# Merging three mixers' branches: later row preparation, a fixed place for one half, a pause before weight scales

## The chip, the cores and the metric

One core of a Trainium2 chip runs the program. The metric is device time in microseconds (us) of one execution. An execution was profiled as well; its span runs from its first to its last instruction.

## What is computed

One macaron block over 1024 tokens of width 1024 (`DEPTH` is 1), all in float32 at the interface:

```python
x = x + 0.5 * swiglu_ffn(rms_norm(x, ffn1_norm[l]), ffn1_w_in[l], ffn1_w_out[l])
h = rms_norm(x, mix_norm[l])
...
o_a = indexed_sparse_attention(...) @ w_o_a[l]
glu_a, glu_b = jnp.split(y_s @ w_glu[l], 2, axis=-1)
o_b = glu_a * jax.nn.sigmoid(glu_b)
o_m = memory_attention(q_m, m_k, m_v) @ w_o_m[l]
g = jax.nn.sigmoid(gates.reshape(b_, s_, N_BRANCHES, D_MODEL))
merged = g[:, :, 0] * o_a + g[:, :, 1] * o_b + g[:, :, 2] * o_m
x = x + merged @ w_out[l]
x = x + 0.5 * swiglu_ffn(rms_norm(x, ffn2_norm[l]), ffn2_w_in[l], ffn2_w_out[l])
x = rms_norm(x, final_norm[l])
```

The place that matters here is `merged` and the product with `w_out` behind it.

## The kernel before

Every operand of a product is held as two float16 halves, a high and a low one, each scaled by a power of two, and a product is three matmuls (`matmul3`): high by high, high by low, low by high. So weights and activations have to be split before TensorE can use them. For a weight block (`WBlock`) this is: load into the staging tile `wf`; square sums per block or per row (ACT writes `junk` and a sum, some on DVE); `weigh` (DVE, `wj`), which weighs the sums by what the activation rows were scaled with; `scale`, which begins with a matmul by ones (tile `ms`) that adds over partitions, and goes on with three to five tiny DVE steps (`wsc`, `wrs`); then the high half (ACT, `wh`) and the low half (DVE, `wh`). For activations, `Rows` does the same: `put(k, src)` starts a generator `steps` whose first part is the square sum on ACT (`junk` with `rsc`), the next, at a later call of `more()`, the power of two on DVE (`rsc`, `mi`, `mj`) and the high half on ACT (`m`), and the last the low half on DVE (`m`).

All instructions are recorded through one helper (line 62), so rows are told apart by tile names. The order on each engine is fixed when the program is built. Generators yield between pieces of TensorE work; a model of the engines' clocks (`Model`) decides which goes on (`Sched`), and after each step `Stream.prep` pushes the weight blocks ahead as far as the model thinks they are ready. `WBlock.can` allows `scale` only once the model's time is `LATE` past the end of the step before; `LATE` is 0.0 until the second FFN sets it to 2.5. Whoever needs a block whose steps have not been issued forces them with `go()` (in `Stream.begin`). On the chip each engine runs its own list in order.

**The merge** (in `mixer`). Channels come in 8 groups d of 128, tokens in 2 halves of 512: 16 units n = 2d + half. A unit has 30 matmuls of 512 columns: six into `gb` (bank tag `lg`), six into `ga` (`mm`), six into `pm` (`ao`), twelve into `po` (`mm`). ACT empties them: tanh of `gb` to `sb`, a copy of `ga` to `gc`, a copy of `pm` to `sm`; in the next unit, behind its first six matmuls, `rest` copies `po` to `m`, a place in `xa`. DVE multiplies `sb` by `gc` and by a gate, `sm` by its gate, `m` by its gate; POOL adds `sm` to `sb` and `sb` to `m`. The three gates come back from DRAM by a DMA on POOL's queue (`g_in`, two units ahead). Temporaries `sb`, `sm`, `gc` share a ring of four buffers (`t2`). Banks: `lg` 2, `mm` 2, `ao` 1, `ms` 3. After the second half of a d, `rest` puts row d into `w["m"]` at once, so the row's square sum stands on ACT right behind the copy of `po`.

`xa` is 16 places of 512 floats: gates in places 0 to 8, `m` in 9 to 14.

**The output projection** (`out_stage`). Weight blocks `out[0]` to `out[3]` of 256 columns (d = 0, 1; 2, 3; ...). The first two are cut into rows 0 to 5 and rows 6 and 7, so that the product can start without the last rows. Tiles go d0, d1, d2 for both halves, then d3 to d7 of half 0, then d3 to d7 of half 1; each is 18 + 6 or 24 matmuls, emptied by DVE into `xo` and `xa`, squared by ACT (`sq`) and summed by DVE (`ss`). `begun` calls `more()` after each pair of rows. Meanwhile the first blocks of the second FFN are prepared (`wf<-in_ffn_w_in_dram`, square sums `junk`), and `norm_forms` norms the finished half (DVE `xa`, ACT and DVE `F`).

Of the kernel before, what the change touches and what calls it, by code (L numbers as in the profile page):

```python
# [21 lines left out]
HT = 512  # L22
# [482 lines left out]
class Stream:  # L505
# [28 lines left out]
    def room(self):  # L534
        return len(self.ring) < 3 or self.ring[-3].uses == 0
# [24 lines left out]
class Rows:  # L560
# [6 lines left out]
        self.inv2 = kb.const.tile([P, nk], F32, name=tag + "j")  # L567
        self.n, self.at, self.late, self.apart = 0, {}, [], False

    def put(self, k, src, mul=None):  # L570

        self.late += [self.steps(k, src, mul)]
        self.more()

    def more(self):
# [4 lines left out]
        while self.late:  # L580
            self.more()

    def steps(self, k, src, mul):
        kb, nc = self.kb, self.kb.nc
        t = kb.small.tile([P, 3], F32, name="rsc", tag="rsc", bufs=4)
        hl = self.t[k] = self.room(k)
        nc.scalar.activation(kb.junk(S), src, AF.Square, accum_out=t[:, 0:1])
        yield None
        kb.pow2(t[:, 0:1], t[:, 1:2], t[:, 2:3])
        inv = self.inv[:, k:k + 1]  # L590
        if mul is None:
            nc.vector.tensor_scalar(inv, t[:, 1:2], INV_MUL, None, op0=OP.mult)
        else:
            nc.vector.tensor_scalar(inv, t[:, 1:2], INV_MUL, mul, op0=OP.mult, op1=OP.mult)
        nc.vector.tensor_tensor(self.inv2[:, k:k + 1], inv, inv, op=OP.mult)
        if self.apart:
            yield None
        nc.scalar.activation(hl[:, 0], src, AF.Copy, scale=t[:, 2:3])
        yield None
        nc.vector.scalar_tensor_tensor(hl[:, 1], src, t[:, 2:3], hl[:, 0], op0=OP.mult, op1=OP.subtract)  # L600
        self.n, self.at[k] = k + 1, nc.t["vector"] + 0.12
# [5 lines left out]
class Builder:  # L607
# [406 lines left out]
    def ffn_strassen(self, name, rows, a, b, F, ring, early, chunks, xd):  # L1014
# [42 lines left out]
        def body(s, then):  # L1057
# [5 lines left out]
            if late:  # L1063
                put(*late.pop())
# [94 lines left out]
        for f in range(PLAIN, NF):  # L1159
            s = s or (yield from first(f))  # L1160
            s = yield from body(s, none if f + 1 == NF or f in ends else lambda: first(f + 1))
            if f in ends:
                rows.flush()
                yield from out(b[ends.index(f)], *chunks[ends.index(f)])
        rows.flush()
        put(*late.pop())
        rows.flush()

# [1046 lines left out]
    def mixer(self, w, xa, ss, xd_in, xd_out, after):  # L2215
# [87 lines left out]
        heads = lambda t, half: lambda i, k: t[:, 4 * half:4 * half + 4, 2 * k + i]  # L2303
        gates, mt, xf = {}, {}, xa.rearrange("p k a h t -> p (k a h t)")
        room = lambda i, n: xf[:, i * HT:(i + n) * HT].rearrange("p (j t) -> p j t", j=n)

        def g_in(n):
            if n < 2 * ND:
                gates[n] = room(3 * (n % 3), 3)
                nc.gpsimd.dma_start(gates[n], gd[:, n // 2, n % 2].rearrange("j p t -> p j t"))  # L2310
# [5 lines left out]
        for n in range(2 * ND):  # L2316
            d, half = divmod(n, 2)
            b = w["go"][d // 2]
            glu, wm, wa = b.segs
            c = (d % 2) * P  # L2320
            yield from self.stream.begin(b)
            gb, ga = self.bank("lg"), self.mm()
            self.matmul3(gb, lambda i, k: glu.hl[:, i, k, 256 + c:256 + c + P], w["y"].x(half), 2)
            if late:
                late.pop()()
            yield None
            self.matmul3(ga, lambda i, k: glu.hl[:, i, k, c:c + P], w["y"].x(half), 2)
            sb, sm, gc = self.t2("sb"), self.t2("sm"), self.t2("gc")
            nc.scalar.activation(sb, gb, AF.Tanh, scale=glu.inv)
            yield None  # L2330
            w["m"].more()
            g_in(n + 2)
            ta, tg, tm = (gates[n][:, j] for j in range(3))
            pm, po = self.bank("ao"), self.mm()
            self.matmul3(pm, lambda i, k: wm.hl[:, i, k, c:c + P], heads(qmS, half), 2)
            nc.scalar.activation(gc, ga, AF.Copy, scale=glu.inv)
            nc.vector.scalar_tensor_tensor(sb, sb, 1.0, gc, op0=OP.add, op1=OP.mult)
            nc.vector.scalar_tensor_tensor(sb, tg, 1.0, sb, op0=OP.add, op1=OP.mult)
            yield None
            self.matmul3(po, lambda i, k: wa.hl[:, i, k, c:c + P], heads(qS, half), 4, ks=range(2))  # L2340
            nc.scalar.activation(sm, pm, AF.Copy, scale=wm.inv)
            nc.vector.scalar_tensor_tensor(sm, tm, 1.0, sm, op0=OP.add, op1=OP.mult)
            nc.gpsimd.tensor_tensor(sb, sb, sm, op=OP.add)
            w["m"].more()
            yield None
            self.matmul3(po, lambda i, k: wa.hl[:, i, k, c:c + P], heads(qS, half), 4, ks=range(2, 4))
            self.stream.end(b)
            if half == 0:
                mt[d] = room(9 + 2 * (d % 3), 2)

            def rest(d=d, half=half, wa=wa, po=po, ta=ta, sb=sb):
                m = mt[d][:, half]
                nc.scalar.activation(m, po, AF.Copy, scale=wa.inv)
                nc.vector.scalar_tensor_tensor(m, ta, 1.0, m, op0=OP.add, op1=OP.mult)
                nc.gpsimd.tensor_tensor(m, m, sb, op=OP.add)
                if half == 1:
                    w["m"].put(d, mt[d].rearrange("p h t -> p (h t)"))

            late.append(rest)
            yield None  # L2360
        w["out"][0].go(("split", 0))
        late.pop()()
        self.stream.BACKLOG = 3
        nc.free.add(xa.tensor.name)
        en.close()
# [212 lines left out]
```

## Time and profile before

| what | value |
|---|---|
| three runs, median (lowest to highest) | 2257.52 us (2257.22 to 2260.11) |
| the profiled execution, its own time | 2257.12 us |
| its span | 2255.0 us, 33448 instructions |
| mean granted TensorE clock | 0.988 |
| busy: PE, DVE, ACT, POOL | 2140.5, 1347.8, 1186.8, 396.2 us |
| HBM read and written | 143.57 and 40.50 MB, 82 GB/s over the span |

Names: PE is TensorE's matmuls, DVE VectorE, ACT ScalarE, POOL GpSimd, SP the queue of SyncE. In a timeline a row is: start in us from the span's start, how long, engine, line, operation, out<-in, shape, count, and in brackets how long the engine had been idle before it and who released it. In a list of waits the time is summed. A matmul's time in the timeline includes its drain, so that of a group overlaps the next.

### The profile page before, as it was taken

How to read it: one execution, taken by the hardware profiler on the slowest of the kernel's cores; microseconds unless marked ns; L12 is line 12 of the kernel's file. 1: busy time of each engine (PE TensorE's matmuls, PEld its weight loads, DVE VectorE, ACT ScalarE, POOL GpSimd, SP SyncE). 2: the span in 40 equal slices, each digit the busy share in tenths (PEclk: the TensorE clock that was granted, in tenths of full speed). 3: DMA queues.
4: the chain of work that ended last, by engine and by line, in shares of the span. 5: the costliest groups of instructions: out<-in, count | busy, mean ns of one | idle time of the engine just before them, and what ended most of it. 6: DMA issues, size and time to landing. Idle time of an engine off the chain costs nothing. (4 is left out here: it accounts for less than half of the span.)

```text
span 2255.0 us, 33448 instructions
## 1 busy us (share of the span) xinstructions
PE 2140.5 (95%) x12585; PEld 1141.1 (51%) x12589; DVE 1347.8 (60%) x3669; ACT 1186.8 (53%) x2367; POOL 396.2 (18%) x582
## 2 busy tenths in 40 slices
PE   6999999999999889979999999898999999999997
PEld 3555444444444556656556674333854444444443
DVE  6446852344555467677669886675756643466653
ACT  6543434344444488778877766544555432455421
POOL 1200130000000103312200004410254301344100
PEclk9999999999999999999999999999999999999999
DMA  6422231202222102123321204334111234112222
GB/s 224 120 82 82 64 103 57 63 26 80 89 89 85 52 20 79 40 66 108 122 86 58 65 37 152 117 120 119 43 57 57 70 123 125 47 57 64 81 62 93
DMA packets 204066, 185.18 MB, mean 82 GB/s; under 512 B 7376, under 2 KB 176528, under 8 KB 203264
## 3 DMA queue, kind: packets, MB, share of 16 engines
q1 hardware_dynamic: 185904, 135.84, 19.1%
q0 software_dynamic: 8416, 29.36, 4.1%
q10 hardware_dynamic: 9584, 17.85, 2.7%
q8 instruction: 98, 1.61, 0.3%
q14 instruction: 64, 0.52, 0.1%
HBM read 143.57 MB, written 40.50 MB: 82 GB/s over the span
## 5 line engine op out<-in xcount | busy, mean ns | idle before, releaser
L62 PEld LDWEIGHTS <-wh 128*128 128x128 f16 x8412 | 817.3, 98 | 949.5 <-issue 38.0
L62 PE MATMUL mm<-xa,wh 128*128 128x512 f16 x2376 | 540.0, 380 | 6.5 <-ACT xa L62 4.9
L62 PE MATMUL lg<-xa,wh 128*128 128x512 f16 x1080 | 242.6, 379 | 0.4 <-DVE xn L62 0.4
L62 ACT ACTIVATE junk<-wf 128x1024 f16<-128x1024 f32 (+3 forms) x292 | 194.0, 664 | 35.7 <-DMA wf<-in_ffn_w_in_dram 20.1
L62 PE MATMUL mm<-G,wh 128*128 128x512 f16 x960 | 210.5, 379 | 0.0
L62 DVE SCALAR_TENSOR_TENSOR wh<-wf,wsc,wh 128x1024 f16<-128x1024 f32 (+1 forms) x132 | 176.3, 1337 | 49.3 <-ACT wh L62 49.1
L62 PE MATMUL mm<-H,wh 128*128 128x512 f16 x864 | 197.3, 383 | 6.8 <-ACT wh L62 5.2
L62 PE MATMUL lg<-F,wh 128*128 128x512 f16 (+1 forms) x900 | 179.4, 353 | 0.0
L62 ACT ACTIVATE wh<-wf,wrs 128x128 f16<-128x128 f32 (+2 forms) x304 | 112.4, 438 | 103.4 <-DVE wrs L62 94.0
L62 ACT ACTIVATE wh<-wf,wsc 128x1024 f16<-128x1024 f32 (+1 forms) x132 | 139.1, 1060 | 33.3 <-DVE wsc L62 23.3
L62 PE MATMUL mm<-wh,xa 128*128 128x256 f16 (+2 forms) x1152 | 129.1, 271 | 13.9 <-ACT us L62 7.8
L62 PE MATMUL mm<-F,wh 128*128 128x512 f16 (+1 forms) x672 | 129.2, 347 | 0.0
L62 PEld LDWEIGHTS <-xa 128*128 128x128 f16 x1152 | 108.2, 106 | 32.1 <-issue 15.4
L62 DVE SCALAR_TENSOR_TENSOR wh<-wf,wrs,wh 128x128 f16<-128x128 f32 (+2 forms) x304 | 112.9, 423 | 12.7 <-ACT wh L62 11.5
L62 DVE SCALAR_TENSOR_TENSOR gt<-lg,wsc,si 128x512 f32<-128x512 f32 x44 | 33.0, 749 | 129.6 <-PE lg L62 110.5
L62 PE MATMUL ao<-F,wh 128*128 128x512 f16 x456 | 104.6, 379 | 0.0
L62 ACT ACTIVATE junk<-wk,kathr 128x1024 f16<-128x1024 f32 (+2 forms) x96 | 99.5, 1036 | 8.7 <-POOL kathr L62 6.8
L62 POOL TENSOR_TENSOR xa<-hs,xa 128x512 f16<-128x512 f32 x16 | 19.9, 1249 | 475.4 <-ACT xa L62 475.4
L62 DVE SCALAR_TENSOR_TENSOR xo<-mm,wsc,xo 128x512 f32<-128x512 f32 x44 | 33.0, 749 | 102.9 <-PE mm L62 102.9
L62 POOL TENSOR_TENSOR xa<-xa 128x512 f32<-128x512 f32 (+1 forms) x40 | 57.2, 1432 | 174.2 <-ACT xa L62 125.7
L62 ACT ACTIVATE junk<-gt 128x1024 f16<-128x1024 f32 x22 | 23.2, 1057 | 120.1 <-DVE gt L62 120.1
L62 PE MATMUL mm<-m,wh 128*128 128x512 f16 x336 | 79.9, 395 | 5.1 <-DVE wh L62 3.2
(511 smaller groups left out, 2924.8 us busy)
## 6 DMA issues: line engine op xcount, KB each, us to landing
wf<-in_ffn_w_in_dram SPq DMA_DIRECT2D x88, 512.0 KB, 4.8
xo<-xd ACTq DMA_DIRECT2D x64, 256.0 KB, 2.7
gd<-gt SPq DMA_DIRECT2D x48, 256.0 KB, 2.0
xa<-gd POOLq DMA_DIRECT2D x16, 768.0 KB, 5.0
wf<-in_ffn_w_out_dram SPq DMA_DIRECT2D x8, 1280.0 KB, 5.9
wf<-in_ffn_w_out_dram SPq DMA_DIRECT2D x7, 1408.0 KB, 5.9
wf<-in_w_in_dram SPq DMA_DIRECT2D x17, 512.0 KB, 4.8
xd<-xa SPq DMA_DIRECT2D x32, 256.0 KB, 2.4
```

Source lines behind the costliest of these rows:

```text
L62: r = f(*a, **k)
```

## The change

Rows are put two steps of a unit later (behind `sm` instead of behind the first six matmuls), `gc` gets place 15 of `xa` for its own instead of a buffer of the ring, the last row's first step waits for three more calls of `more()`, and `LATE` is set to 2.0 from unit 12 on and to 3.5 after the loop. The second FFN sets `LATE` to 2.5 in both kernels once its first three blocks are through.

```diff
@@ -567,9 +567,9 @@
         self.inv2 = kb.const.tile([P, nk], F32, name=tag + "j")
         self.n, self.at, self.late, self.apart = 0, {}, [], False
 
-    def put(self, k, src, mul=None):
-
-        self.late += [self.steps(k, src, mul)]
+    def put(self, k, src, mul=None, after=0):
+
+        self.late += [self.steps(k, src, mul, after)]
         self.more()
 
     def more(self):
@@ -580,8 +580,10 @@
         while self.late:
             self.more()
 
-    def steps(self, k, src, mul):
+    def steps(self, k, src, mul, after):
         kb, nc = self.kb, self.kb.nc
+        for _ in range(after):
+            yield None
         t = kb.small.tile([P, 3], F32, name="rsc", tag="rsc", bufs=4)
         hl = self.t[k] = self.room(k)
         nc.scalar.activation(kb.junk(S), src, AF.Square, accum_out=t[:, 0:1])
@@ -2303,6 +2305,7 @@
         heads = lambda t, half: lambda i, k: t[:, 4 * half:4 * half + 4, 2 * k + i]
         gates, mt, xf = {}, {}, xa.rearrange("p k a h t -> p (k a h t)")
         room = lambda i, n: xf[:, i * HT:(i + n) * HT].rearrange("p (j t) -> p j t", j=n)
+        spare, ready = xf[:, 15 * HT:16 * HT], []
 
         def g_in(n):
             if n < 2 * ND:
@@ -2319,13 +2322,15 @@
             glu, wm, wa = b.segs
             c = (d % 2) * P
             yield from self.stream.begin(b)
+            if n == 12:
+                WBlock.LATE = 2.0
             gb, ga = self.bank("lg"), self.mm()
             self.matmul3(gb, lambda i, k: glu.hl[:, i, k, 256 + c:256 + c + P], w["y"].x(half), 2)
             if late:
                 late.pop()()
             yield None
             self.matmul3(ga, lambda i, k: glu.hl[:, i, k, c:c + P], w["y"].x(half), 2)
-            sb, sm, gc = self.t2("sb"), self.t2("sm"), self.t2("gc")
+            sb, sm, gc = self.t2("sb"), self.t2("sm"), spare
             nc.scalar.activation(sb, gb, AF.Tanh, scale=glu.inv)
             yield None
             w["m"].more()
@@ -2342,6 +2347,8 @@
             nc.vector.scalar_tensor_tensor(sm, tm, 1.0, sm, op0=OP.add, op1=OP.mult)
             nc.gpsimd.tensor_tensor(sb, sb, sm, op=OP.add)
             w["m"].more()
+            if ready:
+                w["m"].put(*ready.pop())
             yield None
             self.matmul3(po, lambda i, k: wa.hl[:, i, k, c:c + P], heads(qS, half), 4, ks=range(2, 4))
             self.stream.end(b)
@@ -2354,12 +2361,14 @@
                 nc.vector.scalar_tensor_tensor(m, ta, 1.0, m, op0=OP.add, op1=OP.mult)
                 nc.gpsimd.tensor_tensor(m, m, sb, op=OP.add)
                 if half == 1:
-                    w["m"].put(d, mt[d].rearrange("p h t -> p (h t)"))
+                    ready.append((d, mt[d].rearrange("p h t -> p (h t)")))
 
             late.append(rest)
             yield None
         w["out"][0].go(("split", 0))
         late.pop()()
+        w["m"].put(*ready.pop(), after=3)
+        WBlock.LATE = 3.5
         self.stream.BACKLOG = 3
         nc.free.add(xa.tensor.name)
         en.close()
```

Three places show how the change moves instructions.

First, ACT in units 4 and 5 of the merge, before the change. `junk_14650,rsc_14648` is the square sum of row 1, `m_14649` its high half; `sb`, `gc`, `sm` are copies out of banks of unit 4, then of unit 5; `xa_91<-mm` is `rest`.

```order
L62 ACTIVATE xa_91<-mm_14610,wsc_12915 128x512
L62 ACTIVATE junk_14650,rsc_14648<-xa_91 128x1024
L62 ACTIVATE sb_14661<-lg_14637,wsc_13129 128x512
L62 ACTIVATE m_14649<-xa_91,rsc_14648 128x1024
L62 ACTIVATE gc_14663<-mm_14638,wsc_13129 128x512
L62 ACTIVATE sm_14662<-ao_14671,wsc_13245 128x512
L62 ACTIVATE xa_91<-mm_14672,wsc_13371 128x512
```

The same with the change (`gc` is now the `xa_91` that reads the bank filled by the second six matmuls: `mm_14634`, `mm_14697`):

```order
L62 ACTIVATE xa_91<-mm_14607,wsc_12915 128x512
L62 ACTIVATE sb_14653<-lg_14633,wsc_13129 128x512
L62 ACTIVATE junk_14658,wrq_14657<-wf_14423 128x512
L62 ACTIVATE xa_91<-mm_14634,wsc_13129 128x512
L62 ACTIVATE junk_14672,wrq_14657<-wf_14423 128x512
L62 ACTIVATE sm_14654<-ao_14661,wsc_13245 128x512
L62 ACTIVATE junk_14685,rsc_14683<-xa_91 128x1024
L62 ACTIVATE junk_14688,wss_14687<-wf_14423 128x512
L62 ACTIVATE xa_91<-mm_14662,wsc_13371 128x512
L62 ACTIVATE sb_14713<-lg_14696,wsc_13129 128x512
L62 ACTIVATE junk_14717,wss_14716<-wf_14423 128x1024
L62 ACTIVATE m_14684<-xa_91,rsc_14683 128x1024
```

The square sum of row 1 moved from in front of `sb` to behind `sm` of unit 4, its high half from in front of `gc` of unit 4 to in front of `gc` of unit 5.

Second, DVE at the end of tile d2 and around tile d3 of the projection, where block `out[2]` is scaled: before the change (`wj_15667` to `wrs_15675`, then `wh_15698`).

```order
L62 SCALAR_TENSOR_TENSOR wj_15667,wss_15578<-wrq_15579,mj_110 128x8
L62 TENSOR_SCALAR wsc_15669<-ms_15670 128x1
L62 TENSOR_SCALAR wsc_15669<-wsc_15669 128x1 x2
L62 TENSOR_SCALAR wrs_15675<-mi_109,wsc_15669 128x8
L62 SCALAR_TENSOR_TENSOR xo4_15399<-mm_15644,wsc_15476,xo4_15399 128x512
L62 SCALAR_TENSOR_TENSOR xa_91<-lg_15678,wsc_15570,xo4_15399 128x2x256
L62 TENSOR_TENSOR ss1_93<-ss1_93,sq_15688 128x512
L62 SCALAR_TENSOR_TENSOR wh_15698<-wf_15494,wrs_15675,wh_15698 128x256 x2
L62 SCALAR_TENSOR_TENSOR junk2_15713,wrq_15710<-wf_15612 128x256
L62 SCALAR_TENSOR_TENSOR xo4_15400<-mm_15691,wsc_15476,xo4_15400 128x512
```

With the change (`wj_15704` to `wrs_15716`, then `wh_15718`; `lg_15691` is the last bank before the block's first product):

```order
L62 SCALAR_TENSOR_TENSOR xo4_15401<-mm_15661,wsc_15309,xo4_15401 128x512
L62 SCALAR_TENSOR_TENSOR xa_91<-lg_15691,wsc_15509,xo4_15401 128x2x256
L62 TENSOR_TENSOR ss0_92<-ss0_92,sq_15701 128x512
L62 SCALAR_TENSOR_TENSOR wj_15704,wss_15594<-wrq_15595,mj_110 128x8
L62 SCALAR_TENSOR_TENSOR junk2_15708,wrq_15673<-wf_15544 128x256
L62 TENSOR_SCALAR wsc_15710<-ms_15711 128x1
L62 TENSOR_SCALAR wsc_15710<-wsc_15710 128x1 x2
L62 TENSOR_SCALAR wrs_15716<-mi_109,wsc_15710 128x8
L62 SCALAR_TENSOR_TENSOR wh_15718<-wf_15527,wrs_15716,wh_15718 128x256 x8
```

The scale of `out[2]` moved from two tiles ahead of the block's first product to behind the last tile before it.

Third, PE in the last two tiles, where the matmul by ones of an FFN block stands (`mm_16092` is tile d6 and `mm_16115` tile d7 of half 1). Before the change, after 18 of the 24 matmuls of tile d6:

```order
L62 MATMUL mm_16092<-m_15139,wh_15822 128x512
L62 LDWEIGHTS ones_b_76
L62 MATMUL ms_16120<-wss_16114,ones_b_76 128x1
L62 LDWEIGHTS ones_b_76
L62 MATMUL ms_16120<-wss_16114,ones_b_76 128x1
L62 LDWEIGHTS wh_15822
```

With the change, after 12 of the 24 matmuls of tile d7:

```order
L62 MATMUL mm_16115<-m_14952,wh_15812 128x512
L62 LDWEIGHTS ones_b_76
L62 MATMUL ms_16131<-wss_16098,ones_b_76 128x1
L62 LDWEIGHTS ones_b_76
L62 MATMUL ms_16131<-wss_16098,ones_b_76 128x1
L62 LDWEIGHTS wh_15812
```

The pair moved back by 6 + 12 = 18 matmuls. The next pair moved by 24 and the one after it by 48 matmuls of 256 columns; behind PE's row 18200 or so (the fourth FFN block) both lists are the same.

## Rows read from the trace of the kernel before

**Rows 1.** The page, part 1: busy us, share, instructions.
```profile
PE 2140.5 (95%) x12585; PEld 1141.1 (51%) x12589; DVE 1347.8 (60%) x3669; ACT 1186.8 (53%) x2367; POOL 396.2 (18%) x582
```

**Rows 2.** Windows: stretch, length, busy us by engine (x), clock, DMA.
```profile
1352.70:1471.00 118.30, 105.35 (x489) 46.83 (x487) 81.86 (x143) 66.97 (x117) 57.38 (x43) 1.00 0.39 129
...
1558.00:1577.00 19.00, 10.25 (x39) 4.43 (x39) 9.22 (x15) 7.83 (x12) 2.31 (x2) 0.73 0.19 55
```

**Rows 3.** Waits of PE, 1352 to 1497 us: total, times, longest.
```profile
PE mm L62 <- ACT gc L62: 9.8, 6, 2.7
```

**Rows 4.** Waits of PE, 1497 to 1645 us.
```profile
PE ms L62 <- ACT junk L62: 10.9, 5, 7.7
```

**Rows 5.** Timeline of PE in the merge: units 0, 1, 5, the end.
```profile
1352.67 1.46 PE L62 MATMUL lg<-y,wh 128*128 128x512 f16 x6
...
1359.15 1.46 PE L62 MATMUL lg<-y,wh 128*128 128x512 f16 x6
...
1387.67 1.46 PE L62 MATMUL mm<-y,wh 128*128 128x512 f16 x6 [1.11 <-ACT gc L62]
...
1471.01 1.24 PE L62 MATMUL mm<-m,wh 128*128 128x512 f16 x5
```

**Rows 6.** Timeline of ACT in the merge: unit 1, unit 4.
```profile
1363.32 0.69 ACT L62 ACTIVATE sm<-ao,wsc 128x512 f32<-128x512 f32 x1 [0.69 <-PE ao L62]
...
1384.28 1.06 ACT L62 ACTIVATE junk<-xa 128x1024 f16<-128x1024 f32 x1 [4.77 <-POOL xa L62]
...
1386.95 0.67 ACT L62 ACTIVATE gc<-mm,wsc 128x512 f32<-128x512 f32 x1
```

**Rows 7.** Timeline of DVE in the merge.
```profile
1360.07 0.69 DVE L62 SCALAR_TENSOR_TENSOR xa<-xa 128x512 f32<-128x512 f32 x1 [1.56 <-ACT xa L62]
...
1389.66 1.28 DVE L62 SCALAR_TENSOR_TENSOR m<-xa,rsc,m 128x1024 f16<-128x1024 f32 x1
...
1390.85 1.76 DVE L62 SCALAR_TENSOR_TENSOR xa<-xa 128x512 f32<-128x512 f32 x1
```

**Rows 8.** Timeline of POOL in the merge.
```profile
1360.90 1.27 POOL L62 TENSOR_TENSOR xa<-xa,sb 128x512 f32<-128x512 f32 x1 [1.05 <-DVE xa L62]
...
1389.84 2.23 POOL L62 TENSOR_TENSOR sb<-sb,sm 128x512 f32<-128x512 f32 x1 [4.85 <-DVE sm L62]
```

**Rows 9.** Timeline of PE, start of the projection.
```profile
1476.30 7.90 PE L62 MATMUL mm<-m,wh 128*128 128x512 f16 x28 [2.84 <-DVE wh L62]
...
1484.62 1.46 PE L62 MATMUL mm<-m,wh 128*128 128x512 f16 x6 [0.42 <-DVE xo L62]
```

**Rows 10.** Timeline of PE, first products of block out[2].
```profile
1515.68 6.94 PE L62 MATMUL mm<-m,wh 128*128 128x512 f16 x30 [0.61 <-ACT wh L62]
...
1522.46 0.17 PE L62 MATMUL ms<-wss,ones_b 128*128 128x1 bf16 x1
```

**Rows 11.** Timeline of DVE at that place.
```profile
1513.81 0.75 DVE L62 SCALAR_TENSOR_TENSOR xa<-lg,wsc,xo 128x512 f32<-128x512 f32 x1 [0.54 <-PE lg L62]
...
1515.26 0.69 DVE L62 TENSOR_TENSOR ss<-ss,sq 128x512 f32<-128x512 f32 x1 [0.69 <-ACT sq L62]
```

**Rows 12.** Timeline of ACT, first high halves of out[3].
```profile
1523.40 0.91 ACT L62 ACTIVATE wh<-wf,wrs 128x256 f16<-128x256 f32 x2 [1.92 <-DVE wrs L62]
```

**Rows 13.** Timeline of PE, end of the projection and second FFN.
```profile
1565.73 0.16 PE L62 MATMUL ms<-wss,ones_b 128*128 128x1 bf16 x1 [7.75 <-ACT junk L62]
...
1566.91 0.16 PE L62 MATMUL ms<-wss,ones_b 128*128 128x1 bf16 x1 [1.02 <-ACT junk L62]
...
1566.94 9.49 PE L62 MATMUL mm<-m,wh 128*128 128x512 f16 x30
...
1594.68 0.16 PE L62 MATMUL ms<-wss,ones_b 128*128 128x1 bf16 x1 [0.95 <-ACT junk L62]
...
1597.71 2.62 PE L62 MATMUL mm<-F,wh 128*128 128x256 f16 x12
```

**Rows 14.** Timeline of DVE, the emptying of tile d5 of half 1.
```profile
1562.20 0.74 DVE L62 SCALAR_TENSOR_TENSOR xa<-mm,wsc,xo 128x512 f32<-128x512 f32 x1
```

## The prediction

> **What bounds the kernel.** I read the page first, then PE by stretches, then the waits of PE, then single rows. PE is busy for 95% of the span [rows 1], so the time is what PE works plus what it waits; a change that adds no matmul can only move the waits. In the merge PE works 105.4 of 118.3 us [rows 2]. The list of waits names the cause: PE stood 9.8 us, in six pieces, for ACT's copy `gc` [rows 3], and later 10.9 us for ACT's square sums of weights [rows 4]. The order of ACT's list says why, and the rows say how much.
>
> **1. The merge.** A unit takes PE 1359.15 - 1352.67 = 6.48 us when nothing is in its way [rows 5]: 30 matmuls, 0.216 us each. Sixteen make 103.7 us; the stage took 1471.01 - 1352.67 = 118.3 [rows 5]. So 14.6 us are lost. The row of unit 4 shows how: ACT stood 4.77 us before the square sum of row 1, for POOL's last addition [rows 6], and behind it in the list were `sb`, the high half and `gc`, which ended at 1386.95 + 0.67 = 1387.6. PE began the second six matmuls of unit 5 at 1387.67, 1.11 us late [rows 5]. Unit 4 began at 1352.67 + 4 x 6.48 = 1378.6, so the row was ready 5.7 us into the unit. With about 3.3 us of ACT work up to the end of `gc` and PE asking 7.8 us into the unit (6.48 + 1.30), anything later than 4.5 stops PE.
>
> The change puts the square sum behind `sm`. In an undisturbed unit (start 1359.15) `sm` starts 4.2 us in [rows 6] and POOL's addition to `m` ends at 1360.90 + 1.27 [rows 8], 3.0 us in: the row is there before ACT asks. What now stands behind the square sum is the copy of `po`, wanted 10.4 us in (6.48 and 18 matmuls), and after the DVE's scale step and the high half the `gc` of the next unit, wanted 14.3 us in (12.96 + 1.30). From the square sum to the end of that `gc` I count some 6 us, so the row may be ready 8 us into the unit, not 4.5. The place of its own for `gc` adds no instruction; it takes `sm`'s wait for POOL's addition out, as two units now share the ring of four. Its reuse is safe by some 5 us: DVE has read it about 4.1 us into a unit (12 matmuls, 2.6, then a copy and a product of 0.7 each) and ACT writes it again 9.2 us in.
>
> What is left is DVE. One of its operations took 1.76 us while POOL was at work, against 0.69 alone [rows 7], and POOL's 2.23 against 1.27 [rows 8]; they take turns. Two units hold on DVE eight operations of 0.69, one of 1.28 [rows 7] and small ones of some 0.6, and on POOL four of 1.27: 5.5 + 1.3 + 0.6 + 5.1 = 12.5 us if none overlap, of 12.96 us on PE. Weight halves come on top, so DVE falls back by a few us in units 5 to 9 and 14 to 15, within the 8 us allowed. I leave 2.0 us of waits: **gain 12.6** (14.6 if DVE keeps up; 6.6 if 8 us stay, about half).
>
> **2. Into the projection.** From 1471.01 [rows 5] to 1484.62 [rows 9] PE did 36 matmuls, 7.8 us of work, in 13.6: 5.8 lost, to a wait of 2.84 for low halves of `out[0]`, one before it, one of 0.42 and 28 matmuls that took 7.90 instead of 6.05 + 0.17 us [rows 9]. With the change those low halves for rows 0 to 3 stand earlier, but I find four new short waits by laying the new lists beside the durations of rows 6 to 8: `gc` of unit 15 behind the high half of row 6, which waits for DVE (2.1 us until its bank is free for the first tile); rows 4 and 5 of `out[0]`, whose low halves stand behind the low half of row 6 (1.5); the first tile, emptied behind four low halves of `out[1]` (1.2); an `lg` bank (0.9). The last row, three calls later, adds nothing: its square sum waits for POOL either way, and its first user is six matmuls behind the fourth tile. Sum 5.7: **gain 0.1** (5.8 if none comes; -2 if a further wait of the size of [rows 9] does).
>
> **3. Block `out[2]`.** This is the price of the longer `LATE`. PE waited 0.61 us here [rows 10]. Now the block's `wj` stands on DVE behind the emptying, square and sum of the last tile before it, and PE's matmul by ones right before the block's first product. From the end of that tile: 0.2 until DVE starts, 1.45 to the start of `ss` [rows 11], 0.6 for it, 0.25 for `wj`, 0.1 to PE, 0.94 from the matmul by ones [rows 10] to ACT's first high half [rows 12], 0.45 for that: 4.0 us instead of 0.8. Behind a long wait PE starts slowly: 1.7 us more for 28 matmuls [rows 9], 9.49 - 6.65 = 2.8 us more for 30 after 8.8 us of waiting [rows 13], in a stretch whose granted clock was 0.73 [rows 2], part of it at 1.2 GHz; after 1.11 us nothing [rows 5]. I take 1.8. **Loss 5.0** (3.2 to 6.0). The Trainium skill (TensorE: Matmul & The Clock Gate, Part 1) says that an idle array falls to half its clock and gets it back by work; by that rule 4.0 us would cost as the longest wait does, 2.8, and the loss be 6.0.
>
> **4. Block `out[3]`.** Its matmul by ones stands 6 instead of 12 matmuls ahead, 1.3 us, and 0.94 + 0.45 are needed; later rows queue behind a tile's square as before. **Loss 0.7** (0 to 1.5).
>
> **5. Third FFN block.** The pair by ones waited 7.75 + 1.02 us [rows 13], because its square sums stand on ACT behind the norm of half 0. It moves back 18 matmuls, 3.9 us. Not all helps: after 6 of them (the wait began at 1565.73 - 7.75 = 1558.0; 1.3 more makes 1559.3) tile d7 needs the bank of d5, which DVE emptied at 1562.20 + 0.74 [rows 14]: 3.6 us of waiting. Twelve matmuls bring PE to 1565.5, the square sums end at 1566.9: 1.4 more. So 5.0 instead of 8.8, and some of the slow restart lies under the second wait. **Gain 4.0** (2.9, if the slow clock costs more; 6.6, if none is left).
>
> **6. The next two pairs.** Of the 10.9 us [rows 4], 2.1 are left for them. They move back 24 and 48 matmuls of 256 columns, 2.6 and 5.2 us; the waits go, and with them the slow twelve (2.62 instead of 1.3) [rows 13]. What is late next, the halves `F` of half 1, is as late as before and needed 5 us behind the waits. **Gain 3.8** (2.1 to 3.8).
>
> On SP seven stores still precede the first FFN block's load, and POOL's gate DMAs keep their order: nothing. Behind the fourth FFN block both lists agree; what PE has gained there it keeps.
>
> **Sum:** 12.6 + 0.1 - 5.0 - 0.7 + 4.0 + 3.8 = 14.8 us. The profiled execution took 2257.12, 0.4 under the median of 2257.52. **Forecast 2257.1 - 14.8 = 2242.3 us.** A change of 0.2%, 4.5 us, is what a measurement here can tell from none.
>
> **Rivals.** *A, the merge runs free and restarts are cheap:* part 1 gives 14.6, part 2 3, part 3 loses 3.2. For it: the first four units ran without a wait. Against it: those had few weights to split. 2257.1 - (14.6 + 3 - 3.2 - 0.7 + 4.0 + 3.8) = 2235.6.
>
> *B, DVE and POOL become the bound of the merge:* busy 81.9 and 57.4 of 118.3 us [rows 2], stretched ones included; weights beside 12.5 of 12.96 us per pair leave too little, `gc` comes late again and 7 us stay in part 1, with part 2 at -1. 2257.1 - (7.6 - 1 - 5.0 - 0.7 + 4.0 + 3.8) = 2248.4. The Trainium skill (SBUF — State Buffer, Who interferes with whom) says that a DVE instruction with two SBUF inputs and a GpSimd instruction that reads SBUF exclude each other for the whole instruction; by that rule no pair overlaps and B's count of 12.5 us holds. The stretched rows agree.
>
> *C, slower, the single place:* if DVE lags by more than 5.1 us, ACT stops at every `gc`, in front of all it has to empty, and each unit is paced by half of 12.5 us, plus a `gc` (0.67) [rows 6] and half a POOL addition (0.6) in turn: 7.5 us, 120 for sixteen, 1.7 over before; with part 2 at -2 and parts 3 and 4 at their worst (-7.5) against 2.9 + 2.1: 2257.1 + 1.7 + 2 + 7.5 - 5.0 = 2263.3. Against it: DVE is idle for 36 of 118 us.
>
> *D, the pauses eat the gain:* the merge gives 8, but forced scales cost as much: parts 2 to 4 -2, -6.0, -1.5, and 5 only 2.9, 6 2.1: 2257.1 - 3.5 = 2253.6.
>
> That the change does not act can be ruled out: the lists differ as shown.
>
> **Chances.** Forecast 0.52, A 0.18, B 0.19, C 0.03, D 0.08. Faster by over 0.2%: forecast, A and B, 0.89; D is within 0.2%, 0.08; slower 0.03. The range 2233.5 to 2251 takes in A and B and leaves out C, D and the outer bounds.
>
> **What would show it.** Right: in the merge ACT's square sums wait less than 1 us each for POOL and 16 units take 104 to 107 us; PE waits about 4 us ahead of the first product of `out[2]`; the wait for square sums at the third FFN block is cut into a piece for a DVE emptying and a short one; the pair after it waits for nothing. Wrong: waits of PE for `gc` above 5 us in sum; no wait at `out[2]`; one of 7 us still at the third FFN block.

## The result, and the profile after

The change is faster: 2242.74 us (2239.39 to 2244.73, 4 runs) against 2258.82 (2257.22 to 2262.76, 4 runs) for the kernel before beside it, ratio 0.9923, 95% interval 0.991 to 0.9935. The forecast was 2242.3. The profiled execution of the kernel after took 2241.08 us, with this head of its page:

```profile
span 2239.3 us, 33472 instructions
PE 2141.1 (96%) x12589; PEld 1140.7 (51%) x12589; DVE 1349.9 (60%) x3669; ACT 1188.6 (53%) x2367; POOL 395.4 (18%) x582
```

PE works as long as before (2141.1 us against 2140.5 [rows 1], with 12589 weight loads in both) in a span that is 15.7 us shorter: waits went, as [rows 1] asked. The place is seen in the timeline of PE (start, duration, what, in brackets the wait before it): the first and last unit of the merge, the start of the projection, `out[2]` and `out[3]`, the third FFN block, and the first and third group of 24 products of `F` in the tag `mm`.

```profile
1354.21 1.46 PE L62 MATMUL lg<-y,wh 128*128 128x512 f16 x6
...
1450.78 0.16 PE L62 MATMUL ms<-wss,ones_b 128*128 128x1 bf16 x1 [1.06 <-DVE wj L62]
...
1457.30 2.75 PE L62 MATMUL mm<-qS,wh 128*128 128x512 f16 x12
1461.86 3.18 PE L62 MATMUL mm<-m,wh 128*128 128x512 f16 x14 [1.80 <-ACT xa L62]
1466.59 4.92 PE L62 MATMUL mm<-m,wh 128*128 128x512 f16 x22 [1.55 <-DVE wh L62]
1472.27 6.64 PE L62 MATMUL mm<-m,wh 128*128 128x512 f16 x30 [0.76 <-DVE rsc L62]
...
1504.54 0.16 PE L62 MATMUL ms<-wss,ones_b 128*128 128x1 bf16 x1 [2.31 <-DVE wj L62]
1505.95 10.75 PE L62 MATMUL mm<-m,wh 128*128 128x512 f16 x42 [1.25 <-ACT wh L62]
...
1520.69 6.94 PE L62 MATMUL mm<-m,wh 128*128 128x512 f16 x30 [1.08 <-ACT wh L62]
...
1556.66 4.44 PE L62 MATMUL mm<-m,wh 128*128 128x512 f16 x12 [4.09 <-DVE xa L62]
1560.94 0.19 PE L62 MATMUL ms<-wss,ones_b 128*128 128x1 bf16 x2
...
1563.58 2.78 PE L62 MATMUL mm<-F,wh 128*128 128x256 f16 x24
...
1586.16 2.78 PE L62 MATMUL mm<-F,wh 128*128 128x256 f16 x24
```

Six waits of PE for `gc` [rows 3] have left not one in the merge, where PE now stands once, 1.06 us, for a weight's `wj`. The two waits of 7.75 and 1.02 for square sums [rows 13] became one of 4.09 for an emptying, and the pair after it [rows 4] waits for nothing. New are four waits at the start of the projection and 2.31 and 1.25 us in front of `out[2]`.

The stretch from the first matmul of the merge to the third group of `F` can be cut the same way in every kernel here; its end in the kernel before is this row:

```profile
1602.79 2.78 PE L62 MATMUL mm<-F,wh 128*128 128x256 f16 x24
```

So it took 1602.79 - 1352.67 = 250.12 us before and 1586.16 - 1354.21 = 231.95 after. Cut at PE's last six `lg` matmuls ahead of `out[2]` (1512.32 before, 1500.77 after), at its first matmul by ones for the row sums of `ss`, and at the first `F`, in us:

| kernel | merge, `out[0]`, `out[1]` | `out[2]`, `out[3]` | to the first `F` | to the third `F` | stretch |
|---|---|---|---|---|---|
| before | 159.65 | 29.67 | 34.28 | 26.52 | 250.12 |
| the change | 146.56 | 34.52 | 28.29 | 22.58 | 231.95 |
| the change again (e5) | 146.54 | 34.56 | 28.28 | 22.59 | 231.97 |
| e1, without LATE | 146.39 | 30.06 | 34.06 | 26.53 | 237.04 |
| e2, `gc` in the ring | 148.99 | 34.68 | 28.31 | 22.59 | 234.57 |
| e3, the place alone | 166.68 | 29.27 | 34.29 | 26.71 | 256.95 |
| e6, LATE alone | 164.13 | 30.21 | 28.27 | 22.59 | 245.20 |
| e7, projection free | 146.34 | 29.93 | 29.15 | 22.59 | 228.01 |
| e8, norm later too | 146.35 | 29.92 | 28.84 | 23.07 | 228.18 |
| e9, rows later alone | 148.47 | 30.05 | 32.82 | 24.85 | 236.19 |
| e11, addition on DVE | 149.22 | 34.55 | 28.29 | 22.59 | 234.65 |

The stretch gains 18.2 us where the two spans differ by 15.7 and the medians by 16.1. The rest of the spans lies outside it: the merge began at 1352.67 before and at 1354.21 after, though the order of instructions up to there is the same, and in the other traces between 1352.2 and 1358.4; and from the third group of `F` to the last instruction it took 652.2 us before and 653.1 after. Where the start moves by several us from one execution to the next, the stretch of the one kernel that was traced twice (the change and e5) repeats to 0.02 us, so parts of a few us are read from it below. Between two kernels it still holds the price of slow matmuls behind a wait, which differs by up to 3 us (last section). In run e10 the one profiled execution was disturbed from the first matmul to the last (6947 us) and is left out, so e10 has times but no rows.

### The profile page after: what moved, and what is told of

Same layout as the page of the kernel before. It is cut to its first block, busy times and chain, and to the rows that moved or that the text cites. A ratio compares the mean times of both kernels' runs of the same rounds, so it can differ in the third digit from the quotient of the medians.

```text
span 2239.3 us, 33472 instructions
## 1 busy us (share of the span) xinstructions
PE 2141.1 (96%) x12589; PEld 1140.7 (51%) x12589; DVE 1349.9 (60%) x3669; ACT 1188.6 (53%) x2367; POOL 395.4 (18%) x582
## 5 line engine op out<-in xcount | busy, mean ns | idle before, releaser
L62 PEld LDWEIGHTS <-wh 128*128 128x128 f16 x8412 | 816.2, 98 | 944.3 <-issue 31.5
L62 DVE SCALAR_TENSOR_TENSOR wh<-wf,wrs,wh 128x128 f16<-128x128 f32 (+2 forms) x304 | 115.7, 432 | 16.0 <-ACT wh L62 14.8
L62 ACT ACTIVATE xa<-mm,wsc 128x512 f32<-128x512 f32 x51 | 34.8, 682 | 104.5 <-PE ms L62 60.9
```

Source lines behind the costliest of these rows:

```text
L62: r = f(*a, **k)
```

## The experiments

All ratios are to the kernel before on the same chip (medians there: 2261.07 us for e1 to e4, 2259.95 for e5 to e8, 2260.33 for e9 to e12).

### e1: without the lines on LATE

```diff
-            if n == 12:
-                WBlock.LATE = 2.0
...
-        WBlock.LATE = 3.5
```

> The change without its two lines on LATE (rows later, own place and after=3 stay). Theory (the parts are independent and add): the merge takes 105 to 107 us as after, the way into the projection gains 1 us, and nothing is lost at out[2], since its matmul by ones stands 19 matmuls (4.1 us) ahead of the block's first product; but the third FFN block again waits 7 to 9 us for its square sums and the two pairs behind it about 2 us with 12 slow matmuls. That is about 14 us under the kernel before, 2245 (2243.5 to 2248), 2 to 4 over the whole change. Rival (the longer LATE makes most of the gain, because it takes weight work out of the merge's lists): the merge takes over 111 us and the time is 2250 or more.

Measured: 2247.52 us, ratio 0.9939 (0.9926 to 0.9953). The time is in the theory's range: all of the first column's 13.1 us stay, `out[2]` costs 0.4 us, and the waits for square sums are back:

```profile
1448.82 0.16 PE L62 MATMUL ms<-wss,ones_b 128*128 128x1 bf16 x1 [2.36 <-DVE wj L62]
...
1458.31 2.75 PE L62 MATMUL mm<-qS,wh 128*128 128x512 f16 x12
...
1552.41 0.16 PE L62 MATMUL ms<-wss,ones_b 128*128 128x1 bf16 x1 [7.75 <-ACT junk L62]
1553.60 0.16 PE L62 MATMUL ms<-wss,ones_b 128*128 128x1 bf16 x1 [1.02 <-ACT junk L62]
1553.62 9.27 PE L62 MATMUL mm<-m,wh 128*128 128x512 f16 x30
```

In the stretch LATE is worth 237.04 - 231.95 = 5.1 us: 5.8 and 3.9 from the FFN's part, less 4.5 at `out[2]` and `out[3]`. That is more than the 2 to 4 expected, and the merge is not as after: it took 1458.31 + 2.59 - 1352.22 = 108.7 us, 3.0 more than the change, because PE waited 2.36 us for `wj` instead of 1.06 and the 18 matmuls behind that wait ran slowly. The way into the projection was that much shorter: its first tile waited for nothing, where the change waits 1.80. So in the merge LATE wins 3.0 us and loses 3.2 right behind it.

### e2 and e3: the place, taken away and alone

e2 is the change with the first line, e3 the kernel before with the second (and `spare` defined):

```diff
-            sb, sm, gc = self.t2("sb"), self.t2("sm"), spare
+            sb, sm, gc = self.t2("sb"), self.t2("sm"), self.t2("gc")
...
-            sb, sm, gc = self.t2("sb"), self.t2("sm"), self.t2("gc")
+            sb, sm, gc = self.t2("sb"), self.t2("sm"), spare
```

> The change without the own place: gc goes back to the ring of four that it shares with sb and sm. All else as in the change, and the order on PE is the same. Theory (the later square sum is what counts; the place takes out only a wait of sm for POOL's last addition of the unit before, which ends ahead of sm when nothing is late): the merge takes 105.5 to 108 us, time 2242.5 to 2245. Rival (the place is needed: in the units where POOL is 2 to 4 us late sm now stops ACT in front of the copies that free PE's banks): the merge takes 110 us or more, time 2247 or more.

> The kernel before with the own place for gc alone; rows are put where they were and LATE is as before. Theory: the square sum still stands in front of gc and waits for POOL, so PE's waits for gc stay above 6 us and the merge takes 114 us or more: 2255 to 2259. Rival (sm's wait for POOL in the ring of four was what made ACT late): the waits for gc fall under 3 us, the merge takes under 109 us, 2250 or less.

Measured: e2 2245.16 us, ratio 0.9929 (0.9916 to 0.9943); e3 2264.28, ratio 1.0019 (1.0009 to 1.0029). e2 ends close above its theory's bounds (a merge of 108.1 us, expected up to 108; a time up to 2245) and far from the rival's. Three waits for `gc` come back, 2.3 us; the fourth in the row below, 1.8, is that of the first tile of the projection, which the change has too. `sm` waits for POOL again. Waits of PE up to that tile, then of ACT, in e2's merge (total, times, longest):

```profile
PE mm L62 <- ACT gc L62: 4.1, 4, 1.8
```
```profile
ACT junk L62 <- POOL xa L62: 10.1, 6, 1.9
ACT sm L62 <- POOL sb L62: 5.1, 4, 2.2
```

The order on PE is not quite that of the change, as the expectation had it: the planner (the model that fixes the order when the program is built) put three matmuls by ones 12 to 24 matmuls later.

In e3 the theory's signs came (waits for `gc` above 6 us, a merge of 122.7), but not its time: alone the place costs 6.8 us in the stretch, 4.3 in the merge and the rest in the first blocks behind it. The same two views of e3's merge say what part of it is (its `gc` is called `xa`, the tensor it now lies in):

```profile
PE mm L62 <- ACT xa L62: 12.8, 6, 4.1
PE ms L62 <- DVE wj L62: 3.1, 2, 1.8
```
```profile
ACT junk L62 <- POOL xa L62: 34.4, 7, 6.0
```

In the kernel before the rows for ACT read 31.5 us for `junk` and 8.7 for `sm`, in the order of the list:

```profile
ACT junk L62 <- POOL xa L62: 31.5, 7, 6.1
ACT sm L62 <- POOL sb L62: 8.7, 7, 1.8
```

So the wait of `sm` did go, but it was no bound: the square sums in front of `gc` then waited 2.9 us longer, and PE stood 12.8 instead of 9.8 us for `gc`. The planner also put eight matmuls by ones elsewhere in the merge and the projection; how much of the 6.8 is theirs was not separated.

This is a rival for the change too, since its scales moved as well: the third to fifth matmul by ones of the merge stand behind 246, 312 and 360 matmuls in the kernel before, behind 186, 222 and 246 in the change, and behind 186, 240 and 282 in e3. But e3, with scales nearly as early and rows put early, gains nothing; so earlier scales alone do not explain the gain of the merge.

### e4, e5, e7: can the price at `out[2]` be had back

e4 takes LATE from all blocks with rows; e5 is the change again; e7 takes it from the projection's four blocks alone.

```diff
-        late = self.LATE if f == self.scale else 0.0
+        late = self.LATE if f == self.scale and g.rows is None else 0.0
```
```diff
         WBlock.LATE = 3.5
+        for b in w["out"]:
+            b.LATE = 0.0
```

> The change, but LATE does not hold the scale of weight blocks that are used with rows (the projection's blocks among them), so out[2] and out[3] are scaled 18 and 24 matmuls earlier, and the FFN's blocks stay as in the change. Theory: the waits of 2.3 and 1.25 us at out[2], its slow matmuls (1.5) and the 1.1 at out[3] go, and as the norm of half 0 starts that much earlier, nothing takes it back: 5 us under the change, 2237.5 (2236.5 to 2240). Rival (a wait takes its place: wj now has to come out of DVE earlier, or the third FFN block's wait for the DVE emptying grows by what was won): 2241.5 to 2243.5.

> The change itself once more, beside the three others of this set, as the mark for differences under 5 us. Theory: as before, 0.992 of the kernel before (0.9915 to 0.993), and from the first matmul of the merge to the third group of 24 products of F (1354.21 to 1586.16, 231.95 us in the profile of after) within 0.5 us of that again, whatever the front of the program does. Rival (the stretch itself varies): over 1 us off.

> The change, with LATE set to 0 for the projection's own blocks only; the later output blocks of the FFN, which run e4 freed too and where PE then waited 2.26 and 6.89 us, stay as in the change. Theory (out[2] and out[3] cost the change what the forecast said, and it can be had back): the waits at 1504.5, 1505.9 and 1520.7 us of the change and its slow matmuls go but for one of about 1.9, the first merge matmul to the third group of F takes 227 to 228.5 us instead of 231.95, and behind it the waits are those of the change: 3.5 to 5 us under the change. Rival (a wait behind takes it back): within 1.5 us of the change.

Measured: e4 2242.21 us, ratio 0.9918 (0.9904 to 0.9932); e5 2242.14, ratio 0.992 (0.9907 to 0.9934); e7 2237.43, ratio 0.9899 (0.9885 to 0.9912). In its profile e4's stretch is 227.71 us, 4.2 under the change, as the theory said; but two waits of later blocks, which the edit had freed too, took most of it back:

```profile
1797.67 0.16 PE L62 MATMUL ms<-wss,ones_b 128*128 128x1 bf16 x1 [2.26 <-DVE wj L62]
...
2102.27 0.16 PE L62 MATMUL ms<-wss,ones_b 128*128 128x1 bf16 x1 [6.89 <-DVE wj L62]
```

In the change PE has no wait at the first place and three of 0.75, 3.87 and 0.35 at the second, so 2.26 + 1.92 = 4.2 us more of waiting. From the third group of `F` to the last instruction e4 took 2240.2 - 1584.24 = 656.0 us against 653.1, so 2.8 of the 4.2 us won were lost there. The rival was right on the time, in another place than it named. e7 leaves those blocks alone and keeps the gain: 231.97 - 228.01 = 4.0 us of the stretch, 4.7 of the medians. Of the waits at `out[2]` and `out[3]` one short one is left. The 18 matmuls behind it took 0.3 us more than at full speed, the next 66 ran at full speed. What e7 gives back is at the third FFN block, where the same wait for the emptying has a slower restart (12 matmuls in 5.28 us instead of 4.44):

```profile
1504.57 4.35 PE L62 MATMUL mm<-m,wh 128*128 128x512 f16 x18 [1.91 <-ACT wh L62]
...
1509.06 14.40 PE L62 MATMUL mm<-m,wh 128*128 128x512 f16 x66
...
1552.50 5.28 PE L62 MATMUL mm<-m,wh 128*128 128x512 f16 x12 [4.08 <-DVE xa L62]
```

e7 beats both kernels.

### e6 and e9: LATE alone, and rows later alone

e6 is the kernel before with the three lines that e1 took out; e9 is e1 with `gc` back in the ring.

> The kernel before with the two lines on LATE alone; rows are put where they were, gc in the ring. Theory (parts are independent): in the merge nothing is won (116 us or more), the waits of 7.75 and 1.02 us for square sums at the third FFN block become one of 4 to 5 for a DVE emptying, the two of 0.95 and 1.02 behind it go, and out[2], whose matmul by ones stands 19 matmuls ahead here, waits 1 to 2 us: 5 to 10 us under the kernel before, 8 likeliest. Rival (the pauses at out[2] and out[3] eat it): within 3 us of the kernel before.

> The later put of the rows alone (with after=3 for the last): gc stays in the ring of four, LATE is as before. The stretch counts from the first matmul of the merge to the third group of 24 products of F: 250.12 us in the kernel before, 231.95 in the change, 234.57 in e2, 245.20 in e6. Theory (putting the rows later is worth 245.20 - 234.57 = 10.6 us, with LATE or without): stretch 239.5 (238.5 to 241). Rival (without LATE the place is what carries it, as e1 had it): 243 or more.

Measured: e6 2256.25 us, ratio 0.9983 (0.9974 to 0.9992), 3.7 us under the kernel before and between its two expectations; e9 2248.44, ratio 0.9943 (0.9928 to 0.9957). e9's stretch of 236.19 lies below the theory's 238.5 to 241. Its first two columns gain 10.8 us, as reckoned; the rest of its 13.9 is a faster restart, treated at the end. e6 gains the FFN's 6.0 and 3.9 in full and nothing in the merge (118.25 us against 118.34), and it loses 4.5 in the first blocks behind it, which was not foreseen. Two of its rows there are waits of PE for weight halves on ACT that the kernel before does not have:

```profile
1476.06 0.60 PE L62 MATMUL mm<-m,wh 128*128 128x512 f16 x2 [1.60 <-ACT wh L62]
...
1509.69 1.56 PE L62 MATMUL lg<-m,wh 128*128 128x512 f16 x6 [2.63 <-ACT wh L62]
```

With rows put early, weights that are scaled later come too late out of ACT. So: rows later 13.9 us alone (10.8 without the restart), LATE 4.9 alone and 5.1 on e1, the place -6.8 alone, 2.6 on e2. LATE on e9 is worth 236.19 - 234.57 = 1.6 only, because e9 has the fast restart already. Each of these numbers includes what the planner moved besides.

### e8 and e12: what is late behind the 4.09 us

```diff
-            yield pace() if half else pace(4.0)
+            yield pace() if half else pace(1.5)
```

This, on e7, puts the last group of the norm of half 0 behind the emptying on DVE; e12 has 7.0 in place of LATE's 3.5 besides.

> e7, and DVE's last group of the norm of half 0 behind the emptying of the tile that PE waits for (4.09 us in the change). Theory: that wait shrinks to 1 to 1.6 us, but the square sums of the third FFN block stand on ACT behind that group, so PE waits some 3 us for them 18 matmuls later: 0 to 1.5 us under e7. Rival (DVE's norm was the only cause, and the square sums are there in time): 3 us or more under e7.

> e8 with LATE of 7.0 instead of 3.5 behind the merge: the pair by ones of the third FFN block now stands 22 products into F, 18 matmuls of 512 columns and 22 of 256 behind the emptying that PE waits for. Theory: the 2.51 and 1.02 us for square sums go and only the 1.38 for the emptying stays, stretch 224.5 (224 to 226) against 228.18, and nothing behind it takes it back. Rival (F's own halves of half 0, or the scale of the block, are late next): 227 or more.

Measured: e8 2236.93 us, ratio 0.9897 (0.9882 to 0.9912), no different from e7; e12 2242.17, ratio 0.9921 (0.9907 to 0.9936), stretch 230.18. The waits moved on, as e8's theory and e12's rival had it. PE in e8, then in e12:

```profile
1552.85 4.04 PE L62 MATMUL mm<-m,wh 128*128 128x512 f16 x18 [1.38 <-DVE xa L62]
1559.41 0.16 PE L62 MATMUL ms<-wss,ones_b 128*128 128x1 bf16 x1 [2.51 <-ACT junk L62]
1560.59 0.16 PE L62 MATMUL ms<-wss,ones_b 128*128 128x1 bf16 x1 [1.02 <-ACT junk L62]
```
```profile
1557.03 2.78 PE L62 MATMUL mm<-F,wh 128*128 128x256 f16 x24 [1.14 <-DVE xa L62]
...
1563.22 1.86 PE L62 MATMUL ms<-ones,ss 128*128 128x1 f32 x8 [3.38 <-DVE ss L62]
```

### e10: the last row at once

```diff
-        w["m"].put(*ready.pop(), after=3)
+        w["m"].put(*ready.pop())
```

> The change, but the last row is put with after=0. Theory (as the prediction had it, the square sum waits for POOL either way and its first user is far behind): stretch 231 to 233 us against 231.95. Rival (the square sum now stands ahead of four weight halves of the projection on ACT, and waits some 4.5 us for POOL's last addition in front of them, so that PE stands for low halves of the first blocks): 234 to 237.

Measured: 2244.57 us (median of the three undisturbed executions, 2244.32 to 2246.88), ratio 0.9934 (0.9918 to 0.9951). That is some 3 us over e5's ratio of 0.992 and leans to the rival, but the intervals overlap and there are no rows, so it stays open.

### e11: the last addition on DVE

```diff
-                nc.gpsimd.tensor_tensor(m, m, sb, op=OP.add)
+                nc.vector.tensor_tensor(m, m, sb, op=OP.add)
```

> The change, with the last addition of each unit (m and sb) on DVE instead of POOL. Theory (DVE and POOL take turns, so a POOL addition of 1.27 us costs DVE more than one of its own of 0.69): ACT's square sums wait less than 8 us in sum in the merge, against 13.2, PE waits no more than in the change, stretch 231 to 233. Rival (DVE becomes the bound with 16 operations more, 11 us): PE waits for gc in the merge, 3 us or more, stretch 235 or more.

Measured: 2245.61 us, ratio 0.9935 (0.9918 to 0.9951), stretch 234.65, 2.7 us longer: out of the theory's range and 0.35 short of the rival's. The rival is nearer on the time but not right on the cause. PE does wait for `gc` again (here `xa`: 2.2 us in three pieces in the merge, and 2.4 instead of 1.8 at the first tile), but DVE is no busier over the merge (84.1 us in e11, 84.2 in the change). Waits of PE in e11 up to the first tile:

```profile
PE mm L62 <- ACT xa L62: 4.6, 4, 2.4
PE ms L62 <- DVE wj L62: 1.8, 1, 1.8
```

Groups of DVE in the merge (busy, mean ns, idle before), the change and then e11:

```profile
L62 DVE SCALAR_TENSOR_TENSOR sb<-xa,sb 128x512 f32<-128x512 f32 x15 | 13.2, 882 | 0.5
L62 DVE TENSOR_TENSOR mj<-mi 128x1 f32<-128x1 f32 x6 | 4.3, 724 | 0.2
```
```profile
L62 DVE TENSOR_TENSOR xa<-xa,sb 128x512 f32<-128x512 f32 x15 | 10.4, 692 | 2.6 <-POOL sb L62 1.2
L62 DVE SCALAR_TENSOR_TENSOR sb<-xa,sb 128x512 f32<-128x512 f32 x15 | 10.4, 692 | 0.5
L62 DVE TENSOR_TENSOR mj<-mi 128x1 f32<-128x1 f32 x6 | 1.0, 159 | 0.2
```

The 10.4 us that DVE took over it saved, for the most part, on products that POOL no longer holds up. What got worse is the order: the addition stands on DVE in front of the row's scale and the next unit's products, and ACT's waits for a row's scale rose from 10.8 us in the change to 14.7.

## Why the prediction was right

**Merge and into the projection, 12.6 + 0.1 forecast, 13.1 measured.** PE's last twelve matmuls end the merge at 1457.30 + 2.59 = 1459.89, 105.7 us after its start; 118.34 - 105.68 = 12.7 for part 1. The mechanism is the one argued. ACT with its list after:

```profile
1384.31 0.69 ACT L62 ACTIVATE sm<-ao,wsc 128x512 f32<-128x512 f32 x1
1386.99 1.06 ACT L62 ACTIVATE junk<-xa 128x1024 f16<-128x1024 f32 x1 [2.00 <-POOL xa L62]
```

The square sum still waits for POOL (8.7 us in the merge, 31.5 before), but behind `sm`, and PE does not notice. That each such wait would be under 1 us was wrong: 2.00, 1.54, 3.07, 2.07 and, for the last row, 4.55. In the merge the room of 8 us carried it, by little: of the square sums that waited for POOL the latest began at 1440.63, 7.9 us into its unit (1432.72). Of the 2.0 us over sixteen free units, 1.06 is a wait, and it is for `wj`, not for `gc`. The four waits foreseen at the projection came with 1.80, 1.55, 0.76 and 0.90 us, for 2.1, 1.5, 1.2 and 0.9. (The third is for the first tile's emptying, 1471.47 + 0.74 on DVE, though the row names `rsc`, DVE's next instruction.)

Two things in these parts were not as argued. That the last row adds nothing is not shown: ACT stood the 4.55 us ahead of two high halves of weights, and DVE did two low halves behind them just before the emptying that PE waited 0.76 us for; the run that puts the last row elsewhere (e10) left no rows. And the split between the parts came out with the help of LATE, which the prediction counted only as a price: without it (e1) part 1 gains 118.3 - 108.7 = 9.7 and the way to `out[2]` 3.6. The sum is the same, 13.3.

**`out[2]` and `out[3]`, -5.7 forecast, -4.85 measured.** PE's first product of `out[2]` came 1505.95 - 1502.06 = 3.89 us late (4.0 foreseen; the six `lg` matmuls from 1500.77 on end at 1502.06), its 42 matmuls took 10.75 us, some 1.5 more than at full speed (1.8), and `out[3]` waited 1.08. e7 showed that this price is LATE's and not the rows'.

**Third FFN block, 4.0 forecast, 6.0 measured.** This is the term that was mis-sized. The emptying was late by 4.1 us instead of 3.6, but the second wait, 1.4, did not come: the twelve matmuls in between ran slowly, 4.44 us instead of 2.75, and the last square sum had ended on ACT at 1560.54, ahead of the matmul by ones at 1560.94. Slow matmuls and the wait lay over one another; the forecast counted nearly all of both.

**The next two pairs, 3.8 forecast, 3.9 measured.** Both waits are gone, and so are the slow matmuls behind them. The terms that the prediction gives for it add up to less than 3.8: 2.62 - 1.47 = 1.15 for the slow twelve (with the drain on both sides), and 2.1 for the waits. The rest is a second slow twelve in the kernel before, 2.03 - 1.47 = 0.56:

```profile
1595.89 2.03 PE L62 MATMUL mm<-FB,wh 128*128 128x256 f16 x12
```

In the stretch the sum is 18.2 against 14.8: a gain of 2.0 too little at the FFN block, 0.9 too much cost at `out[2]` and `out[3]`, 0.5 elsewhere. That the median agrees to 0.4 us with the forecast is partly luck. The stretch gained 3.4 us more than forecast, start and end of the profiled execution took 1.5 and 0.9 us longer than those of the kernel before, and the forecast started from 2257.1, 1.7 under the median of 2258.82 that the kernel before had beside the change.

Rival A's free merge came half true (no wait for `gc`), B's bound did not: in the merge PE stood 1.06 us for DVE and nothing for `gc`. C named the single place as a danger; alone it does make the kernel slower (e3), though by no stop of ACT at `gc` but by what stood before. What D named, scales in the way of the rest, shows in e6 alone, where 9.9 us are gained behind and 5.0 given back in the projection.

## What to carry to other kernels

Move a step that waits for a slow engine behind the copies the busy engine needs next, and count how late its input may come: here 8.7 us of such waits stayed in the merge, and PE did not wait for them. Where three edits go together, try each alone and on top of the others: the place costs 6.8 us alone and gains 2.6 behind the later rows, and as the planner moves other steps with every edit, such a number is the edit's and not the line's. A pause that helps one kind of block should be given to that kind only (e7), and the gain of a few us is to be read between two fixed instructions of two traces, not from the total.

## What the runs showed of the hardware

**The price of a restart is not fixed.** e1 and e9 reach the third FFN block with the same waits in the same order; the rows of e1 stand above, these are e9's:

```profile
1554.66 0.16 PE L62 MATMUL ms<-wss,ones_b 128*128 128x1 bf16 x1 [7.75 <-ACT junk L62]
1555.84 0.16 PE L62 MATMUL ms<-wss,ones_b 128*128 128x1 bf16 x1 [1.02 <-ACT junk L62]
1555.87 8.04 PE L62 MATMUL mm<-m,wh 128*128 128x512 f16 x30
```

Thirty matmuls took 8.04 us there and 9.27 in e1; at full speed they take 6.64. At the next pair it is plainer: behind waits of 0.95 and 1.02 us in both, the granted clock was 0.72 over six us in e1 (part of them at 1.2 GHz) and 1.00 in e9 (all at 2.4). The twelve matmuls after them took 2.26 us in e1 and the next twelve 2.40, and in e9 1.47 each. These are six-microsecond windows of e1 and then of e9 (length, then busy time of PE, its weight loads, DVE, ACT and POOL, then PE's granted clock, DMA share, GB/s):

```profile
1581.00:1587.00 6.00, 4.83 (x30) 3.64 (x30) 4.58 (x10) 3.46 (x8) 2.03 (x2) 0.72 0.01 3
```
```profile
1582.00:1588.00 6.00, 4.83 (x45) 4.28 (x45) 4.58 (x10) 3.46 (x8) 2.04 (x2) 1.00 0.01 3
```

So a forecast should hold a range for it: here 0 to 1.7 us for waits of 2 us in sum, 1.4 to 2.8 for 8.8 (the kernel before has the 2.8). The Trainium skill (TensorE: Matmul & The Clock Gate, Part 1) says that the number of slow matmuls at a start differs between runs of one kernel. No run here shows that: these rows are of two kernels with the same order at that place, and the one kernel traced twice repeated its stretch to 0.02 us.

**DVE and POOL take turns even for a tiny operation.** In the change DVE's product of two columns of 128 numbers took 1.09 us while POOL added, and 0.16 on average in e11, where the addition is not on POOL; a one-input operation right before it, also while POOL added, took 0.14. DVE and then POOL in the change:

```profile
1443.81 0.14 DVE L62 TENSOR_SCALAR mi<-rsc 128x1 f32<-128x1 f32 x1
1443.99 1.09 DVE L62 TENSOR_TENSOR mj<-mi 128x1 f32<-128x1 f32 x1
```
```profile
1443.79 1.27 POOL L62 TENSOR_TENSOR xa<-xa,sb 128x512 f32<-128x512 f32 x1 [0.69 <-DVE rsc L62]
```

The product ended with POOL's addition, at 1445.1. The Trainium skill (SBUF — State Buffer, Who interferes with whom) says that a DVE instruction with two SBUF inputs is shut out for the whole of a GpSimd instruction that reads SBUF, and one with a single input, outside its two-port modes, is not; the trace agrees in these two operations, 1.09 and 0.14 us. Such an operation on the way to a row's scale costs not its 0.16 us but what is left of POOL's.
